# Holding back the first stores of an all-to-all dispatch kernel with a GpSimd copy

## The chip, the cores and the metric

The kernel runs on one core of a Trainium2 chip. The metric is the time of one execution on the device in microseconds (us). Before the change the median of three runs is 239.9 us (239.7 to 240.48).

The core has a matrix engine (TensorE, not used here), VectorE (DVE in the profile), ScalarE (ACT), GpSimd (POOL) and SyncE (SP). 16 DMA engines move data between HBM and the on-chip memory SBUF, which has 128 partitions. SP and ScalarE each have a DMA queue here; a transfer is issued by an instruction in the stream of the engine that owns the queue.

## The reference

Each of 16 x 1024 = 16384 tokens has a row of 512 float32 values and two weights. The output holds each row twice, once times each weight. The expert indices are an input and are not used.

```python
x_expanded = x[:, :, np.newaxis, :].repeat(k, axis=2)   # k = 2
weights = expert_weights[..., np.newaxis]
return (x_expanded * weights).astype(np.float32)
```

So 33.5 MB of x and 0.13 MB of weights are read, and 67.1 MB are written.

## The kernel before

Each of the 128 partitions handles 128 tokens. They are cut into five tiles of 25 tokens per partition and a last small one of 3. "Token" below means one token in each of the 128 partitions: 256 KB of x, 512 KB of output.

**Memory.** Two buffers of 25 tokens hold x (tile 0, 2 and 4 use the one, tile 1 and 3 the other), `z_tile` holds x of the last 3 tokens, `w_tile` holds all weights, and one buffer `o_ring` holds the output of one whole tile. All later tiles write into the same `o_ring`, so a part of it can be computed again only when its earlier store has landed.

**Products.** A tile is done in two halves, of 13 and 12 tokens. In `fill` VectorE takes the first tokens of a half (9 in tile 0, 8 later), four tokens an instruction (line 116), and ScalarE the others, one output row of 512 an instruction (line 106). When a half is done, SP issues its store (line 141).

**Loads.** ScalarE's queue carries x (line 79). Tile 0 comes in two steps of 9 and 16 tokens. Tile 1 is issued right behind, but in the compiled order its issue waits until the first 9 tokens have landed. Tile 2 is issued when both engines are done with tile 0. The load of the three last tokens (line 87) stands behind tile 2's load on ScalarE's queue; a one-column copy (line 76), which writes `z_tile` and reads the last column of `o_ring`, keeps it behind tile 0's products. Tile 3 and 4 are issued when their buffers are free.

**Weights.** SP's queue carries six loads of weights (line 93), one for each tile and one for the last three tokens, all issued at the start. The stores go into the same queue behind them. Each weight load is 128 pieces of 200 bytes (24 bytes for the last three tokens).

The order of each engine's instructions is the order of the program; semaphores between engines and DMAs are put in by the framework from the overlaps of the buffers.

Of the kernel before, what the change touches and what calls it, by code (L numbers as in the profile page):

```python
# [1 line left out]

# [4 lines left out]


@with_exitstack
def kernel(  # L10
    ctx: ExitStack,
    tc: tile.TileContext,
    x: bass.AP,
    expert_indices: bass.AP,
    expert_weights: bass.AP,
    out: bass.AP,
):
    nc = tc.nc

    batch, seq, hidden = x.shape  # L20
    k = expert_weights.shape[-1]
    P = nc.NUM_PARTITIONS
    ntok = batch * seq
    assert ntok % P == 0
    A_TOTAL = ntok // P

    f32 = mybir.dt.float32
    row = k * hidden
    CH = 4


    groups = [25, 25, 25, 25, 25]
    TX = max(groups)
    LAST = 3
    FIRST = [9, 16]
    SHARES = [[9, 9], [8, 8]]
    assert sum(groups) + LAST == A_TOTAL

    xf = x.rearrange("b s h -> (b s) h")
    of = out.rearrange("b s k h -> (b s) (k h)")  # L40
    wf = expert_weights.rearrange("b s k -> (b s) k")

    w_pool = ctx.enter_context(tc.tile_pool(name="w_pool", bufs=1))
    x_pool = ctx.enter_context(tc.tile_pool(name="x_pool", bufs=2))
    o_pool = ctx.enter_context(tc.tile_pool(name="o_pool", bufs=1))

    w_tile = w_pool.tile([P, A_TOTAL * k], f32)
    o_ring = o_pool.tile([P, TX * row], f32)

    def rows(of_all, done, T):  # L50
        return of_all[done * P : (done + T) * P, :].rearrange(
            "(p a) n -> p (a n)", a=T
        )


    if LAST:
        z_pool = ctx.enter_context(tc.tile_pool(name="z_pool", bufs=1))
        z_tile = z_pool.tile([P, LAST * hidden], f32)

    tiles = []  # L60
    done = 0
    for n in groups:
        tiles.append((done, n))
        done += n

    loaded = []

    def load(i):
        if i >= len(tiles):
            return  # L70
        done, n = tiles[i]
        x_tile = x_pool.tile([P, TX * hidden], f32)
        src = rows(xf, done, n)
        steps = FIRST if i == 0 else [n]
        if i == 2 and LAST:
            nc.scalar.copy(out=z_tile[:, :1], in_=o_ring[:, TX * row - 1 :])  # L76
        for e, step in enumerate(steps):
            at = sum(steps[:e])
            nc.scalar.dma_start(  # L79
                out=x_tile[:, at * hidden : (at + step) * hidden],  # L80
                in_=src[:, at * hidden : (at + step) * hidden],
            )
            if i == 0 and e == 0:
                for g in range(len(tiles) + 1):
                    weights(g)
        if i == 2 and LAST:
            nc.scalar.dma_start(out=z_tile, in_=rows(xf, A_TOTAL - LAST, LAST))
        loaded.append(x_tile)


    def weights(e):
        at, n = tiles[e] if e < len(tiles) else (A_TOTAL - LAST, LAST)
        nc.sync.dma_start(
            out=w_tile[:, at * k : (at + n) * k], in_=rows(wf, at, n)
        )

    def product(engine, o_tile, t, x_in, c, m):

        o = t * row
        if engine is not None:  # L100
            for e in range(m * k):
                out_e = o_tile[:, o + e * hidden : o + (e + 1) * hidden]
                in_e = x_in[:, e // k * hidden : (e // k + 1) * hidden]
                w_e = w_tile[:, c + e : c + e + 1]
                if engine is nc.scalar or engine is nc.any and (c + e) % 3 == 2:
                    nc.scalar.mul(out=out_e, in_=in_e, mul=w_e)  # L106
                else:
                    nc.vector.tensor_scalar(
                        out=out_e,
                        in0=in_e,  # L110
                        scalar1=w_e,
                        scalar2=None,
                        op0=mybir.AluOpType.mult,
                    )
            return
        nc.vector.tensor_tensor(  # L116
            out=o_tile[:, o : o + m * row].rearrange(
                "p (t k h) -> p t k h", t=m, k=k
            ),
            in0=x_in[:, : m * hidden]  # L120
            .rearrange("p (t h) -> p t h", t=m)
            .unsqueeze(2)
            .to_broadcast([P, m, k, hidden]),
            in1=w_tile[:, c : c + m * k]
            .rearrange("p (t k) -> p t k", t=m)
            .unsqueeze(3)
            .to_broadcast([P, m, k, hidden]),
            op=mybir.AluOpType.mult,
        )

    def fill(o_tile, x_in, c, m, v):
        for t in range(0, v, CH):
            u = min(t + CH, v)
            product(None, o_tile, t, x_in[:, t * hidden : u * hidden], c + t * k, u - t)
        product(nc.scalar, o_tile, v, x_in[:, v * hidden :], c + v * k, m - v)

    def emit(src, dst, c, cuts, shares):
        for at, to, v in zip(cuts, cuts[1:], shares):
            o_tile = o_ring[:, at * row : to * row]
            fill(o_tile, src[:, at * hidden : to * hidden], c + at * k, to - at, v)  # L140
            nc.sync.dma_start(out=dst[:, at * row : to * row], in_=o_tile)  # L141

    for i in range(2):
        load(i)
    for i, (done, n) in enumerate(tiles):
        emit(loaded[i], rows(of, done, n), done * k, [0, 13, n], SHARES[min(i, 1)])
        load(i + 2)
    emit(
        z_tile,
        rows(of, A_TOTAL - LAST, LAST),  # L150
        (A_TOTAL - LAST) * k,
        [0, LAST],
        [LAST],
    )

# [1 line left out]
_INS = ['x', 'expert_indices', 'expert_weights']  # L157
_OUTS = [((16, 1024, 2, 512), 'float32')]


# [23 lines left out]
```

## Time and profile before

| what | value |
|---|---|
| median of three runs | 239.9 us |
| profiled execution | 239.73 us |
| its span | 238.0 us |
| VectorE busy | 93.2 us |
| ScalarE busy | 55.2 us |
| GpSimd busy | 0.2 us |
| bytes moved by DMA | 100.80 MB |
| mean rate over the span | 424 GB/s |

The profile is that of one execution. Its span runs from the first to the last instruction on the core; the profiled execution's own time is 1.73 us longer than its span. The view of DMA issues gives the median time from issue to landing of a group of transfers, so a transfer that stands behind others in its queue shows a long time. In the 40-slice line a digit is the mean busy share of the 16 DMA engines in tenths. In the timeline each row has a start, a length, the engine (ending in q where the engine only issues a DMA), the line, the operation, and in brackets the idle time ahead of it with what ended it. A DMA view for a stretch of time counts the packets that moved in it by queue: q10 is ScalarE's queue, q1 is SP's.

### The profile page before, as it was taken

Reading aid. Unit: us, or ns where it says so; the run is one execution under the profiler, and the core shown is the slowest. Engines: PE = TensorE matmul, PEld = TensorE weight load, DVE = VectorE, ACT = ScalarE, POOL = GpSimd, SP = SyncE. Lnnn points to the kernel's source line nnn. Section 1 sums busy time; section 2 is a strip of 40 time slices with the busy share of each in tenths; the row PEclk is TensorE's granted clock in tenths of the full one; section 3 lists DMA queues with packets and bytes.
Section 4 is the critical chain, followed back from the end, with each engine's and each line's share of the span. In section 5 each row is a group of like instructions: output and inputs, shape, how many; then the busy total and the mean of one; then the engine's idle time right before and its main releaser. Section 6 shows DMA issues by size and latency. Waiting matters only on the chain.

```text
span 238.0 us, 214 instructions
## 1 busy us (share of the span) xinstructions
DVE 93.2 (39%) x23; ACT 55.2 (23%) x88; POOL 0.2 (0%) x4
## 2 busy tenths in 40 slices
DVE  0599800000059193086005902920085292861300
ACT  0008800000054170081005302700080280800000
POOL 0000000000000000000000000000000000000000
DMA  6999999999999999999999999999999999999996
GB/s 252 445 415 493 475 415 414 415 386 457 430 406 397 434 439 456 458 430 415 405 435 484 430 434 434 413 405 431 490 430 448 417 397 423 457 448 438 438 397 264
DMA packets 3457, 100.80 MB, mean 424 GB/s; under 512 B 1152, under 2 KB 1152, under 8 KB 1280
## 3 DMA queue, kind: packets, MB, share of 16 engines
q1 hardware_dynamic: 2448, 67.24, 65.5%
q10 hardware_dynamic: 1008, 33.55, 33.1%
q14 instruction: 1, 0.01, 0.0%
HBM read 33.69 MB, written 67.11 MB: 424 GB/s over the span
## 4 chain that ended last, share of the span: by engine, by line
DMA 69%; DVE 16%; issue 5%; ACT 3%; ACTq 0%; DVEq 0%; SPq 0%
DMA out_dram<-o_ring 62%; DVE o_ring L116 16%; DMA x_tile<-in_x_dram 7%; ACT o_ring L106 2%; ACT L106 1%; ACTq L79 0%; DVEq L116 0%; SPq L141 0%; ACTq L106 0%
## 5 line engine op out<-in xcount | busy, mean ns | idle before, releaser
L116 DVE TENSOR_TENSOR o_ring<-x_tile,w_tile 128x4096 f32<-128x4096 f32 (+1 forms) x22 | 89.8, 4130 | 122.4 <-DMA out_dram<-o_ring 102.8
L106 ACT ACTIVATE o_ring<-x_tile,w_tile 128x512 f32<-128x512 f32 x86 | 53.7, 708 | 134.4 <-DMA out_dram<-o_ring 134.4
L116 DVE TENSOR_TENSOR o_ring<-z_tile,w_tile 128x3072 f32<-128x3072 f32 x1 | 3.4, 3359 | 7.0 <-DMA out_dram<-o_ring 7.0
L106 ACT ACT_TABLE_LOAD x1 | 1.3, 1283 | 18.8 <-DMA x_tile<-in_x_dram 18.8
L76 ACT COPY z_tile<-o_ring 128x1 f32<-128x1 f32 x1 | 0.2, 191 | 0.0
L168 POOL MEMSET const-bfloat16-1.0<- 128x1 bf16 x1 | 0.1, 102 | 0.0
L168 POOL MEMSET const-uint8-127<- 128x1 uint8 x1 | 0.1, 102 | 0.0
L168 POOL MEMSET const-float32-1.0<- 128x1 f32 x1 | 0.1, 99 | 0.0
L168 POOL MEMSET const-float32-0.0<- 128x1 f32 x1 | 0.1, 98 | 0.2 <-issue 0.2
## 6 DMA issues: line engine op xcount, KB each, us to landing
out_dram<-o_ring SPq DMA_DIRECT2D x5, 6656.0 KB, 32.7
out_dram<-o_ring SPq DMA_DIRECT2D x5, 6144.0 KB, 36.4
x_tile<-in_x_dram ACTq DMA_DIRECT2D x4, 6400.0 KB, 29.7
x_tile<-in_x_dram ACTq DMA_DIRECT2D x1, 4096.0 KB, 17.6
x_tile<-in_x_dram ACTq DMA_DIRECT2D x1, 2304.0 KB, 8.1
out_dram<-o_ring SPq DMA_DIRECT2D x1, 1536.0 KB, 14.6
z_tile<-in_x_dram ACTq DMA_DIRECT2D x1, 768.0 KB, 10.5
w_tile<-in_expert_weights_dram SPq DMA_DIRECT2D x5, 25.0 KB, 24.7
```

The lines of the kernel that those rows point to most:

```text
L76: nc.scalar.copy(out=z_tile[:, :1], in_=o_ring[:, TX * row - 1 :])
L106: nc.scalar.mul(out=out_e, in_=in_e, mul=w_e)
L116: nc.vector.tensor_tensor(out=o_tile[:, o : o + m * row].rearrange("p (t k h) -> p t k h", t=m, k=k), in0=x_in[:, : m * hidden] .rearrange ...
L168: nc = _bacc.Bacc("TRN2", target_bir_lowering=False, num_devices=1)
```

## The change

Three things are changed.

1. The weights of tiles 0 and 1 stay on SP's queue. Those of tiles 2 and 3 (now one transfer), of tile 4 and of the last three tokens are issued on ScalarE's queue, behind tile 1's load.
2. Tile 2 is loaded in two steps, 23 tokens and then 2. It is now issued ahead of the one-column copy, and the load of the three last tokens follows the 2.
3. The two stores of tile 0 are issued only after three small GpSimd copies. The first reads a place that the load of the 23 tokens writes, so it waits until they are in; the second reads two columns of `o_ring`, one in each half, and the third writes the same values back. Each of them passes through the small buffer `hold`, so they run one after the other, and the stores, which read what the third wrote, wait for it.

The buffers of x are now named in a list instead of coming from a pool of two. In the compiled order tile 1's load no longer waits for the first 9 tokens. The products, the shares of the engines, the cuts into halves and all later stores and loads stay.

```diff
-    FIRST = [9, 16]
-    SHARES = [[9, 9], [8, 8]]
+    STEPS = {0: [9, 16], 2: [23, 2]}
...
+    hold = w_pool.tile([P, 2], f32)
+    x_pair = [x_pool.tile([P, TX * hidden], f32, name=f"x{e}") for e in range(2)]
+    z_tile = x_pool.tile([P, LAST * hidden], f32)
...
+    def load(i, e):
+        at = sum(STEPS.get(i, groups[i : i + 1])[:e])
+        to = at + STEPS.get(i, groups[i : i + 1])[e]
+        part = slice(at * hidden, to * hidden)
+        nc.scalar.dma_start(out=x_pair[i % 2][:, part], in_=rows(xf, *tiles[i])[:, part])
...
+    def weights(engine, g, to):
+        at, n = tiles[g]
+        engine.dma_start(
+            out=w_tile[:, at * k : (at + (to - g) * n) * k].rearrange(
+                "p (g m) -> p g m", g=to - g
+            ),
+            in_=wf[at * P : (at + (to - g) * n) * P, :].rearrange(
+                "(g p a) n -> p g (a n)", g=to - g, p=P
+            ),
         )
...
-    for i in range(2):
-        load(i)
+    load(0, 0)
+    weights(nc.sync, 0, 1)
+    weights(nc.sync, 1, 2)
+    load(0, 1)
+    load(1, 0)
+    weights(nc.scalar, 2, 4)
+    weights(nc.scalar, 4, 5)
+    nc.scalar.dma_start(
+        out=w_tile[:, (A_TOTAL - LAST) * k :], in_=rows(wf, A_TOTAL - LAST, LAST)
+    )
     for i, (done, n) in enumerate(tiles):
-        emit(loaded[i], rows(of, done, n), done * k, [0, 13, n], SHARES[min(i, 1)])
-        load(i + 2)
...
+        dst = rows(of, done, n)
+        halves = [(0, 13), (13, n)]
+        for at, to in halves:
+            make(x_pair[i % 2], done * k, at, to, 9 if i == 0 else 8)
+            if i > 0:
+                store(dst, at, to)
+        if i == 0:
+            nc.scalar.copy(out=z_tile[:, :1], in_=o_ring[:, TX * row - 1 :])
+            load(2, 0)
+            load(2, 1)
+            nc.scalar.dma_start(out=z_tile, in_=rows(xf, A_TOTAL - LAST, LAST))
+
+            nc.gpsimd.tensor_copy(out=hold, in_=x_pair[0][:, :2])
+            held = o_ring[:, : 13 * row + 1 : 13 * row]
+            nc.gpsimd.tensor_copy(out=hold, in_=held)
+            nc.gpsimd.tensor_copy(out=held, in_=hold)
+            for at, to in halves:
+                store(dst, at, to)
+        elif i + 2 < G:
+            load(i + 2, 0)
+    make(z_tile, (A_TOTAL - LAST) * k, 0, LAST, LAST)
+    store(rows(of, A_TOTAL - LAST, LAST), 0, LAST)
```

More of the change, by code (lines that the diff above doesn't have):

```diff
@@ L43 @@
     w_pool = ctx.enter_context(tc.tile_pool(name="w_pool", bufs=1))
-    x_pool = ctx.enter_context(tc.tile_pool(name="x_pool", bufs=2))
+    x_pool = ctx.enter_context(tc.tile_pool(name="x_pool", bufs=1))
     o_pool = ctx.enter_context(tc.tile_pool(name="o_pool", bufs=1))
     w_tile = w_pool.tile([P, A_TOTAL * k], f32)
+    hold = w_pool.tile([P, 2], f32)
     o_ring = o_pool.tile([P, TX * row], f32)
+    x_pair = [x_pool.tile([P, TX * hidden], f32, name=f"x{e}") for e in range(2)]
+    z_tile = x_pool.tile([P, LAST * hidden], f32)
     def rows(of_all, done, T):
@@ L53, in rows @@
         )
-    if LAST:
-        z_pool = ctx.enter_context(tc.tile_pool(name="z_pool", bufs=1))
-        z_tile = z_pool.tile([P, LAST * hidden], f32)
     tiles = []
@@ L64 @@
         done += n
[L66 to L94, printed above, removed]
+    def load(i, e):
[12 more added lines that the diff above has]
+            ),
         )
```

20 lines of the change are left out of this document (8 added, 12 removed).

## The prediction

> **What bounds the kernel now.** I read the page first, for who is busy and how many bytes move.
>
> ```profile
> span 238.0 us, 214 instructions
> DVE 93.2 (39%) x23; ACT 55.2 (23%) x88; POOL 0.2 (0%) x4
> DMA  6999999999999999999999999999999999999996
> ...
> DMA packets 3457, 100.80 MB, mean 424 GB/s; under 512 B 1152, under 2 KB 1152, under 8 KB 1280
> ...
> q1 hardware_dynamic: 2448, 67.24, 65.5%
> q10 hardware_dynamic: 1008, 33.55, 33.1%
> ...
> DMA 69%; DVE 16%; issue 5%; ACT 3%; ACTq 0%; DVEq 0%; SPq 0%
> ```
>
> VectorE and ScalarE are mostly idle. The 40-slice DMA line has no slice below 9 between its ends, and the two queues (q1 is SP's, q10 ScalarE's) fill 65.5 + 33.1 = 98.6% of 16 engines' span, 234.7 of 238.0 us. So the chain's "DVE 16%" is not a term of the sum: stores of the other half run meanwhile. The time is bytes over rate, plus moments in which the DMA engines have nothing queued or work badly. The bytes don't change, so only those moments can.
>
> Next the DMA issues and the timeline up to the first stores.
>
> ```profile
> out_dram<-o_ring SPq DMA_DIRECT2D x5, 6656.0 KB, 32.7
> out_dram<-o_ring SPq DMA_DIRECT2D x5, 6144.0 KB, 36.4
> x_tile<-in_x_dram ACTq DMA_DIRECT2D x1, 4096.0 KB, 17.6
> x_tile<-in_x_dram ACTq DMA_DIRECT2D x1, 2304.0 KB, 8.1
> w_tile<-in_expert_weights_dram SPq DMA_DIRECT2D x5, 25.0 KB, 24.7
> w_tile<-in_expert_weights_dram SPq DMA_DIRECT2D x1, 3.0 KB, 49.0
> ```
>
> ```profile
> 0.73 3.11 SPq L93 DMA_DIRECT2D w_tile<-in_expert_weights_dram  x6
> 0.73 8.50 ACTq L79 DMA_DIRECT2D x_tile<-in_x_dram  x3
> ...
> 18.79 1.28 ACT L106 ACT_TABLE_LOAD   x1 [18.79 <-DMA x_tile<-in_x_dram]
> 20.08 8.69 ACT L106 ACTIVATE o_ring<-x_tile,w_tile 128x512 f32<-128x512 f32 x14
> 25.12 197.72 SPq L141 DMA_DIRECT2D out_dram<-o_ring  x11
> 28.80 0.19 ACT L76 COPY z_tile<-o_ring 128x1 f32<-128x1 f32 x1
> 28.86 0.35 ACTq L79 DMA_DIRECT2D x_tile<-in_x_dram  x1
> 41.70 0.33 ACTq L87 DMA_DIRECT2D z_tile<-in_x_dram  x1
> ...
> 68.17 8.76 DVE L116 TENSOR_TENSOR o_ring<-x_tile,w_tile 128x4096 f32<-128x4096 f32 x2 [39.54 <-DMA out_dram<-o_ring]
> ```
>
> A 3 KB transfer that takes 49.0 us to land is the strange row. The weights are issued in SP's first 4 us, yet the last of them lands at about 52. The first store is issued at 25.12, behind them in the same queue. The DMA view by stretch shows what that means: 25 to 48 us, 48 to 52 and 52 to 90.
>
> ```profile
> DMA packets 416, 9.87 MB, mean 429 GB/s; under 512 B 224, under 2 KB 224, under 8 KB 224
> q10 hardware_dynamic: 208, 9.83, 98.9%
> q1 hardware_dynamic: 208, 0.04, 0.8%
> out_dram<-o_ring SPq DMA_DIRECT2D x1, 6656.0 KB, 42.9
> x_tile<-in_x_dram ACTq DMA_DIRECT2D x1, 6400.0 KB, 20.4
> z_tile<-in_x_dram ACTq DMA_DIRECT2D x1, 768.0 KB, 10.5
> ```
>
> ```profile
> DMA packets 416, 1.66 MB, mean 414 GB/s; under 512 B 272, under 2 KB 272, under 8 KB 400
> q10 hardware_dynamic: 160, 0.79, 63.2%
> q1 hardware_dynamic: 256, 0.87, 53.7%
> ```
>
> ```profile
> DMA packets 352, 16.52 MB, mean 435 GB/s; under 512 B 32, under 2 KB 32, under 8 KB 32
> q1 hardware_dynamic: 352, 16.52, 100.3%
> ```
>
> From 25 to 48 us SP's queue moved 0.04 MB in 208 packets, weights only, though a store had been issued at 25.12: small weight packets take turns with 50 KB packets of x, and the store stands behind them. **The stores of the first tile are held today already**, by accident, until the third tile is nearly in: it lands at 28.86 + 20.4 = 49.3, the three-token tile at 41.70 + 10.5 = 52.2. Nor is there a rate to win by separating reads from writes: reads alone run at 429 GB/s, stores alone at 435.
>
> The Trainium skill ("DMA: Bandwidth & Descriptors", section "Queues, rings and completion order") says that each DMA engine takes turns between its queues packet by packet, whatever their size. The trace agrees: 208 weight packets against 208 of x in that stretch.
>
> **The change, part by part.** The sum is made against the profiled execution: 238.0 of span and 1.7 around it, 239.73 us, 0.2 below the median of 239.9.
>
> *Loads.* x of tile 1 no longer waits for the first 9 tokens; they and the next 16 tokens are queued anyway: 0. Tile 2's load is issued, as now, when both engines are done with tile 0, at 20.08 + 8.69 = 28.8. Tile 1's load covers that until about 34.0 (tile 2's 6400 KB need 15.3 us at 429 GB/s before they are in at 49.3). That leaves some 4 us after the 1.0 from issue to first bytes (below); without that cover the loss would be what ScalarE is late. ScalarE's queue now issues six DMAs before its first product, some 0.35 us each by the rows above, all before 4 us; it waits until 18.79 for data. The two extra issues at 28.8 delay no product, since the next ones wait for a store until 68.
>
> *Weights.* The number of transfers and packets stays; four transfers of weights (tiles 2, 3, 4 and the last three tokens), 512 packets, move from SP's queue, where they alternate with x, into ScalarE's queue in one burst between tile 1 and tile 2. Interleaved, 208 cost 0.8% of 23 us = 0.18 us, 14 ns each on one of 16 engines, so 512 cost 0.45 us. In a burst: below, 0.45 us better if they vanish. Above, each packet stalls as the small three-token load does: that load took 63.2% of 4 us = 2.53 us for 0.79 MB that need 1.83 at 429 GB/s, 0.70 us over 8 packets per engine, 87 ns each; 32 packets per engine then cost 2.8 us, 2.35 more than now. The nearest row is the start, where the first weights run in bursts too:
>
> ```profile
> GB/s 0 0 0 0 0 0 5 331 228 151 150 379 149 671 373 373 523 297 447 671 75 664 516 75 745 373 150 670 373 299 745 148 667 1324 132 0 0 924 1055 131
> q1 hardware_dynamic: 240, 0.04, 2.9%
> ```
>
> In 0 to 10 us, 240 packets took 2.9% = 0.29 us, 19 ns each. At that price 512 cost 0.6 us, 0.15 more than now. I take +0.2, with the restart of x behind them.
>
> *The hold.* Tile 2 comes as 23 and 2 tokens. The 2 are 512 KB, 1.2 us at 429 GB/s, so the 23 are in at 49.3 - 1.2 = 48.1. Then three GpSimd copies, each waiting for the one before, and the first store's issue. Every store queues behind this on SP; VectorE's first product of tile 1 waits for the same copies and for the first store anyway; GpSimd has nothing else to do. What such a copy costs is not in the trace; the nearest rows are these.
>
> ```profile
> L116 DVE TENSOR_TENSOR o_ring<-x_tile,w_tile 128x1024 f32<-128x1024 f32 x2 | 2.4, 1216 | 0.0
> L168 POOL MEMSET const-float32-0.0<- 128x1 f32 x1 | 0.1, 98 | 0.2 <-issue 0.2
> ```
>
> Between 0.10 us (GpSimd's own memset) and 1.22 us (VectorE's smallest, with 512 times the elements); I take 0.2 like ScalarE's 128x1 copy (0.19), so 0.6 in all, 0.1 more for hand-over. From issue to first bytes it takes about 1.0 us (weights issued at 0.73, first bytes in the slice at 1.5 to 1.75). So store bytes start at 48.1 + 0.7 + 1.0 = 49.8; with the upper price 48.1 + 3.65 + 1.0 = 52.8. The cover is what stands in ScalarE's queue: 2 + 3 tokens, 1.31 MB, 3.05 us at full rate, until 51.1 at least. Idle time: 0, at the upper price 1.7 us. If nothing covered it, the hold would cost the whole 1.7 us.
>
> *Small loads.* The 2-token load adds 8 packets of 4 KB per engine to the 8 of 6 KB of the three-token load, the kind that wasted 0.70 us. Below: stores come early enough to fill those gaps, and 0.70 us is won. Above: the 2 tokens waste 0.70 as well. The hold lets about 1.7 us of small packets run alone, more than half of them: I take +0.4 for the 2 tokens and -0.2 for the three.
>
> *After that.* Stores begin about where they do now, each half (14 to 16 us) covers the 8.8 us of products of the other, and loads 3 and 4 are issued at the same places. Nothing is gained or lost: 0.
>
> Sum: 239.73 + 0.2 + 0 + 0.4 - 0.2 = 240.1 us: within what a measurement of this kernel can tell from no change (0.3%, 0.7 us: 239.2 to 240.6).
>
> **The rivals.**
> *Faster.* The store's packets come in before the small loads have stalled, and the burst is prefetched behind tile 1's big packets. The 0.70 and the 0.45 go: 239.73 - 1.15 = 238.6. For it: back-to-back weights were cheap at the start. Against: the small loads stand before the store for 1.7 us. It decides if the hold takes under 1 us.
> *The hold outlasts its cover.* GpSimd copies and their semaphores cost 1.2 us each: 1.7 idle and 0.4 of stalled small loads, 241.8. It decides above about 0.65 us a copy ((3.05 - 1.0 - 0.1) / 3). Against it: GpSimd's own 0.10.
> *The burst stalls.* 87 ns a packet instead of 14: 239.73 + 2.35 + 0.2 = 242.3. Against it: the first weights, 19 ns.
> *A small load pays for itself.* The three-token load lands 2.9 us after tile 2's, 1.1 more than its bytes need; the 2-token load pays 1.1 as well: 240.8. The Trainium skill speaks for this one ("DMA: Bandwidth & Descriptors", section "Rules for kernel authors"): it asks for 1 MiB or more per DMA, and this load has half of that. [...]
> *The change does not do what it says*, since the stores are held already: that is the forecast itself.
>
> **How the numbers follow.** Forecast 0.43 (no change); faster rival 0.19; hold too long 0.15; burst 0.12; small load 0.09; 0.02 for a cause that I don't see, shared by both sides. Faster 0.2, same 0.43, slower 0.37. The range runs from the faster rival's 238.6, a little inside it at 238.7, to 242.0, above the hold's 241.8; it leaves out the full burst and a part of the faster case, under 2 in 10.
>
> **What would show it.** Right: no slice below 9 in the DMA line around 48 to 52; the first store's issue some 0.7 us after the 23 tokens land; GpSimd copies of 0.1 to 0.3 us; tile 2's 23 tokens landing near 48; the first products of tile 1 starting near 67 instead of 68. Wrong: an idle stretch of the DMA engines ahead of the first store, or copies over 0.65 us (the hold); 23 tokens landing a microsecond or more later than 48 (the burst); a queue share of ScalarE above 33.1 + 0.4% (small loads); a sum of shares 0.4% below 98.6 with a shorter span (the faster rival). I would be wrong altogether if the rate of the stores alone or of the mixed stretches changed, since no step of mine touches it.

## The result and the profile after

The changed kernel takes 240.93 us (median of 8 runs, 240.64 to 241.61) against 239.87 us (median of 8, 239.61 to 240.48) for the kernel before: a ratio of 1.0045, 95% interval 1.0031 to 1.0058. It is slower by 0.45%. The forecast was 240.1 us and no change; the measured time lies inside its range, above the 239.2 to 240.6 us that counted as no change, on the side that had a chance of 0.37. The profiled execution took 240.83 us, 239.0 of them span. One run of the changed kernel with a delay, below, fell into a slower state (244.66 us) and is left out of its median and ratio.

From the page of the changed kernel, the lines that answer to the first ones above:

```profile
span 239.0 us, 218 instructions
...
DMA  6999998999999999999999999999999999999996
...
q1 hardware_dynamic: 1872, 67.16, 65.2%
q10 hardware_dynamic: 1712, 33.64, 33.4%
```

The DMA engines are as full as before: 65.2 + 33.4 = 98.6% of the span, now of 239.0 us instead of 238.0, for the same bytes. So the extra microsecond isn't a gap in front of the stores. Packets take longer somewhere.

The changed kernel's timeline around the hold:

```profile
28.72 0.33 ACTq L67 DMA_DIRECT2D x<-in_x_dram  x1
...
48.28 0.19 POOL L153 COPY hold<-x 128x2 f32<-128x2 f32 x1 [47.84 <-DMA x<-in_x_dram]
48.52 0.19 POOL L155 COPY hold<-o_ring 128x2 f32<-128x2 f32 x1
48.77 0.19 POOL L156 COPY o_ring<-hold 128x2 f32<-128x2 f32 x1
48.98 0.82 SPq L125 DMA_DIRECT2D out_dram<-o_ring  x2
```

The 23 tokens release GpSimd at 48.28 us, each copy takes 0.19 us, and the first store is issued 0.70 us after the release.

To find where the time goes I use VectorE's starts as milestones. Its first product of a half begins when the store that held that part of the output buffer has landed, so the starts say how far the DMA queues are. First the kernel before, then the changed one (start, length, engine, line, operation; in brackets the idle time ahead and what ended it). The row at 68.17 of the kernel before stands in the prediction.

```profile
82.57 8.76 DVE L116 TENSOR_TENSOR o_ring<-x_tile,w_tile 128x4096 f32<-128x4096 f32 x2 [5.64 <-DMA out_dram<-o_ring]
...
127.88 8.76 DVE L116 TENSOR_TENSOR o_ring<-x_tile,w_tile 128x4096 f32<-128x4096 f32 x2 [17.05 <-DMA out_dram<-o_ring]
...
173.18 8.76 DVE L116 TENSOR_TENSOR o_ring<-x_tile,w_tile 128x4096 f32<-128x4096 f32 x2 [17.13 <-DMA out_dram<-o_ring]
...
219.12 3.36 DVE L116 TENSOR_TENSOR o_ring<-z_tile,w_tile 128x3072 f32<-128x3072 f32 x1 [6.95 <-DMA out_dram<-o_ring]
```

```profile
67.33 8.76 DVE L99 TENSOR_TENSOR o_ring<-x,w_tile 128x4096 f32<-128x4096 f32 x2 [38.69 <-DMA out_dram<-o_ring]
...
81.68 8.76 DVE L99 TENSOR_TENSOR o_ring<-x,w_tile 128x4096 f32<-128x4096 f32 x2 [5.59 <-DMA out_dram<-o_ring]
...
128.41 8.76 DVE L99 TENSOR_TENSOR o_ring<-x,w_tile 128x4096 f32<-128x4096 f32 x2 [17.05 <-DMA out_dram<-o_ring]
...
174.25 8.76 DVE L99 TENSOR_TENSOR o_ring<-x,w_tile 128x4096 f32<-128x4096 f32 x2 [17.45 <-DMA out_dram<-o_ring]
...
220.20 3.36 DVE L99 TENSOR_TENSOR o_ring<-z_tile,w_tile 128x3072 f32<-128x3072 f32 x1 [6.97 <-DMA out_dram<-o_ring]
```

| milestone (us) | before | changed | difference |
|---|---|---|---|
| tile 1, first half | 68.17 | 67.33 | -0.84 |
| tile 1, second half | 82.57 | 81.68 | -0.89 |
| tile 2, second half | 127.88 | 128.41 | +0.53 |
| tile 3, second half | 173.18 | 174.25 | +1.07 |
| last three tokens | 219.12 | 220.20 | +1.08 |

The changed kernel is 0.9 us ahead when the first stores have landed. It then loses 1.42 us between the second halves of tiles 1 and 2 (46.73 us instead of 45.31) and another 0.54 us between those of tiles 2 and 3 (45.84 instead of 45.30). From there both run alike (45.94 and 45.95 us). The two stretches that lose are those in which the loads of tiles 3 and 4 meet the stores.

Call the first of these stretches **the first meeting**. Between the landing of tile 0's second store and that of tile 1's second store, 6656 + 6144 KB of output and 6400 KB of x go through, 19.7 MB. At the 435 GB/s of the stores alone that is 45.2 us. The kernel before needs 45.31, nothing to spare; the changed kernel needs 46.73. In the DMA view of the 15 us in which tile 3's load begins (90 to 105 us), of the kernel before and of the changed one:

```profile
DMA packets 141, 6.45 MB, mean 430 GB/s; under 512 B 16, under 2 KB 16, under 8 KB 16
q1 hardware_dynamic: 87, 3.69, 56.8%
q10 hardware_dynamic: 54, 2.76, 42.5%
```

```profile
DMA packets 132, 6.00 MB, mean 400 GB/s; under 512 B 16, under 2 KB 16, under 8 KB 16
q1 hardware_dynamic: 84, 3.54, 57.4%
q10 hardware_dynamic: 48, 2.46, 43.3%
```

In the second one the shares still add up to 100.7% (99.3% in the first): the engines were busy all the time and moved 400 GB/s. A packet of x took 1.89 us in the first (42.5% of 15 us on 16 engines, for 54 packets) and 2.16 us in the second.

More than half of the 0.9 us gained ahead of that comes from the small loads. From 48 to 51 us in the changed kernel:

```profile
q10 hardware_dynamic: 223, 1.04, 85.7%
```

1.04 MB in 85.7% of 3 us are 405 GB/s while they ran. The three-token load of the kernel before moved 0.79 MB in 2.53 us, 312 GB/s. So the small loads no longer stall. At 405 GB/s their 1.31 MB take 3.24 us; in the kernel before the three tokens took 2.53 us, and the other two, at the 429 GB/s of x, 1.22. That is 0.5 of the 0.9 us. A part of the rest lies in how a milestone is read (see the end of the experiments).

### The profile page after: what moved, and what is told of

Read it like the earlier page. It is cut to its first block, busy times and chain, and to the rows that moved or that the text cites. A ratio compares the mean times of both kernels' runs of the same rounds, so it can differ in the third digit from the quotient of the medians.

```text
span 239.0 us, 218 instructions
## 1 busy us (share of the span) xinstructions
DVE 93.1 (39%) x23; ACT 55.1 (23%) x88; POOL 0.8 (0%) x7
## 2 busy tenths in 40 slices
DMA packets 3585, 100.80 MB, mean 422 GB/s; under 512 B 1152, under 2 KB 1152, under 8 KB 1408
## 3 DMA queue, kind: packets, MB, share of 16 engines
q1 hardware_dynamic: 1872, 67.16, 65.2%
q10 hardware_dynamic: 1712, 33.64, 33.4%
## 4 chain that ended last, share of the span: by engine, by line
DMA 52%; issue 25%; DVE 16%; POOL 0%; POOLq 0%; DVEq 0%; SPq 0%
DMA out_dram<-o_ring 52%; DVE o_ring L99 16%; DVEq L99 0%; POOLq L187 0%; POOL hold L153 0%; POOL hold L155 0%; SPq L125 0%; POOLq L155 0%; POOLq L176 0%
## 5 line engine op out<-in xcount | busy, mean ns | idle before, releaser
L99 DVE TENSOR_TENSOR o_ring<-x,w_tile 128x4096 f32<-128x4096 f32 (+1 forms) x22 | 89.8, 4130 | 123.4 <-DMA out_dram<-o_ring 103.6
L89 ACT ACTIVATE o_ring<-x,w_tile 128x512 f32<-128x512 f32 x86 | 53.7, 708 | 135.2 <-DMA out_dram<-o_ring 135.2
```

What stands on the lines that cost most here:

```text
L99: nc.vector.tensor_tensor(out=o_tile[:, o : o + m * row].rearrange("p (t k h) -> p t k h", t=m, k=k), in0=x_in[:, : m * hidden] .rearrange ...
```

## The experiments

The measure of each is its time against the kernel before on the same chip, and the length of the first meeting, from the two rows of its timeline that are shown: the starts of tile 1's second half (near 82) and of tile 2's second half (near 128). In full-rate terms it is 45.2 us.

### Is it the same every time?

The changed kernel, run again.

> The changed kernel once more, unaltered, for a second trace. In step theory (when tile 3's load starts, most of the 16 DMA engines alternate between a packet of x and a packet of output at the same moment, and such packets take longer): again 13 or so of 16 engines take their first packet of tile 3 about 2 us after the others, and 90 to 105 us again moves about 400 GB/s against 430 before. Rival (a passing disturbance of one execution): the stretch moves 430 GB/s this time, and the time is still 240.9 us for another reason.

One run of 241.06 us, beside 239.69 us for the kernel before. Its DMA view from 90 to 105 us:

```profile
q1 hardware_dynamic: 84, 3.54, 57.1%
q10 hardware_dynamic: 48, 2.46, 43.9%
```

The same packets and bytes as in the first trace. The loss belongs to the kernel, not to one execution.

### Does the moment of tile 3's load matter?

Seven one-column copies on ScalarE between VectorE's last product of tile 1 and the issue of tile 3's load, in the changed kernel; and four in the kernel before.

```diff
         elif i + 2 < G:
+            for _ in range(7 if i == 1 else 0):
+                nc.scalar.copy(out=x_pair[i % 2][:, :1], in_=o_ring[:, 21 * row - 1 : 21 * row])
             load(i + 2, 0)
```

```diff
+        for _ in range(4 if i == 3 else 0):
+            nc.scalar.copy(out=x_tile[:, :1], in_=o_ring[:, 21 * row - 1 : 21 * row])
         for e, step in enumerate(steps):
```

> The changed kernel with seven one-column ScalarE copies between the end of tile 1's products and the issue of tile 3's load, some 1.7 us of delay; nothing else. In step theory: a packet takes 1.97 us, so a delay of 1.7 us puts the issue where about half of the engines take the load one packet earlier than the others, as in the kernel before; the long packets go, 90 to 105 us moves about 430 GB/s, and the time falls by about 1 us to 239.8 us. Rival (the moment does not matter; what stalls is the place in memory or the earlier start of the stores): 240.9 us, 90 to 105 us about 400 GB/s. If a later load simply cost its delay: 242.6 us.

> The kernel before with four such copies ahead of tile 3's load, some 1.0 us of delay. In step theory: half a packet later than now all engines take the load at the same packet, go in step, and the time rises by about 1.2 us to 241.1 us, with the rate from 90 to 107 us down from 430 to about 400 GB/s. Rival (the moment does not matter, the DMA engines are full anyway): 239.9 us and 430 GB/s. Both this and the delayed changed kernel have to come out as in step theory says for it to stand.

Changed kernel with the delay: 240.60 us (five runs), ratio 1.0047 (1.0033 to 1.0060). Its timeline, with the copies:

```profile
81.77 8.76 DVE L99 TENSOR_TENSOR o_ring<-x,w_tile 128x4096 f32<-128x4096 f32 x2 [5.62 <-DMA out_dram<-o_ring]
...
90.56 1.53 ACT L161 COPY x<-o_ring 128x1 f32<-128x1 f32 x7 [3.85 <-DVE o_ring L99]
...
128.63 8.76 DVE L99 TENSOR_TENSOR o_ring<-x,w_tile 128x4096 f32<-128x4096 f32 x2 [19.71 <-DMA out_dram<-o_ring]
```

The load goes out 1.5 us later, and the first meeting takes 46.86 us: the loss stays. Kernel before with the delay: 240.78 us, ratio 1.0043 (1.0028 to 1.0058).

```profile
82.28 8.76 DVE L118 TENSOR_TENSOR o_ring<-x_tile,w_tile 128x4096 f32<-128x4096 f32 x2 [5.64 <-DMA out_dram<-o_ring]
...
91.13 0.86 ACT L76 COPY x_tile<-o_ring 128x1 f32<-128x1 f32 x4 [3.91 <-DVE o_ring L118]
...
127.92 8.76 DVE L118 TENSOR_TENSOR o_ring<-x_tile,w_tile 128x4096 f32<-128x4096 f32 x2 [17.39 <-DMA out_dram<-o_ring]
...
174.82 8.76 DVE L118 TENSOR_TENSOR o_ring<-x_tile,w_tile 128x4096 f32<-128x4096 f32 x2 [18.73 <-DMA out_dram<-o_ring]
```

Here the first meeting takes 45.64 us, 0.33 more than without the delay and 1.1 less than in the changed kernel. The loss of the profiled execution (241.38 us, above the median; the runs spread from 239.79 to 241.66) is at the second meeting, with tile 4's load: 46.90 us against 45.30. So the two runs contradict the in-step theory, as it was put, at the place where it was to hold: the delay did not cure the changed kernel, and it did not bring the loss to tile 3's load in the other one. That a shifted load can make the kernel before 0.4% slower stands; in the one execution that was profiled it is lost at the next load.

### Where do the stores have to meet the loads without the hold?

The three GpSimd copies are left out of the changed kernel.

```diff
-            nc.gpsimd.tensor_copy(out=hold, in_=x_pair[0][:, :2])
-            held = o_ring[:, : 13 * row + 1 : 13 * row]
-            nc.gpsimd.tensor_copy(out=hold, in_=held)
-            nc.gpsimd.tensor_copy(out=held, in_=hold)
```

> The changed kernel without the three GpSimd copies: the first stores go out at about 25 us and alternate with the loads of tiles 1 and 2. In step theory: no fixed gain or loss from the hold as such; the three small loads then stand among stores and do not stall (0.6 us less than the kernel before), while the mixed stretch moves to 26 to 60 us and costs between 0 and 1.5 us by how the engines stand there: 239.3 to 241.0 us. Rival (reads and writes together are slow in themselves): over 241.5 us.

240.76 us, ratio 1.0048 (1.0031 to 1.0065): no better than with the hold. Stores and loads now meet at 25 us. The DMA view from 25 to 32 us:

```profile
DMA packets 48, 2.49 MB, mean 356 GB/s; under 512 B 0, under 2 KB 0, under 8 KB 0
q10 hardware_dynamic: 32, 1.64, 68.2%
q1 hardware_dynamic: 16, 0.85, 28.1%
```

Two packets of x per engine, 1.64 MB, took 68.2% of 7 us = 4.77 us, where 435 GB/s would need 3.77. One microsecond is lost there, at the first place where a large load and a large store meet. The rival that reads and writes are slow together throughout (over 241.5 us) falls.

### Is it where the buffers lie?

The small buffer takes 32 bytes per partition and moves all buffers behind it; the three-token buffer stands elsewhere too. Three kernels: the changed one with 64 bytes instead, the kernel before with 32 unused bytes, and the changed one with every buffer at the address of the kernel before.

```diff
-    hold = w_pool.tile([P, 2], f32)
+    hold = w_pool.tile([P, 16], f32)
...
```

```diff
     w_tile = w_pool.tile([P, A_TOTAL * k], f32)
+    spare = w_pool.tile([P, 2], f32)
+    nc.gpsimd.memset(spare, 0.0)
```

```diff
-    hold = w_pool.tile([P, 2], f32)
...
-    z_tile = x_pool.tile([P, LAST * hidden], f32)
+    z_pool = ctx.enter_context(tc.tile_pool(name="z_pool", bufs=1))
+    z_tile = z_pool.tile([P, LAST * hidden], f32)
+    hold = z_pool.tile([P, 2], f32)
```

(In the first of them the three copies then use `hold[:, :2]`.)

> The changed kernel with its small buffer made 16 columns wide instead of 2. In the changed kernel the buffer takes 32 bytes per partition, and the buffers of x and output behind it start 32 bytes off a multiple of 64; in the kernel before they start on one. With 64 bytes they do again. Place theory (an odd 32 bytes makes packets long where loads and stores alternate): the 1.2 us of long packets at 90 to 105 us go, that stretch moves about 430 GB/s, and since the changed kernel was 1.0 us ahead at 82 us the time is about 239.0 us. Rival (the moment at which the stores and loads meet, which this does not move): 240.9 us and 400 GB/s.

> The kernel before with two unused columns behind the weights (32 bytes), so that its buffers of x and output lie 32 bytes off a multiple of 64 as in the changed kernel; they are cleared once by GpSimd at the start. Place theory: long packets appear where tile 3's load meets the stores, 90 to 107 us falls from 430 to about 400 GB/s, and the time rises by 1 us or more to about 240.9 us. Rival (place does not matter): 239.8 us.

> The changed kernel with the three-token buffer and the small buffer behind the output, so that every buffer has exactly the address that it has in the kernel before; the work and its order are unchanged. Place theory, if it is the order or distance of the buffers and not the 64 bytes that counts: this one falls to about 239.0 us and the padded one does not; if it is the 64 bytes both do. Rival (the moment): both stay at 240.9 us.

In this order: 241.06 us, ratio 1.0060 (1.0044 to 1.0076); 239.78 us, 1.0003 (0.9994 to 1.0011); 240.86 us, 1.0049 (1.0034 to 1.0065). Their timelines, in the same order:

```profile
81.70 8.76 DVE L99 TENSOR_TENSOR o_ring<-x,w_tile 128x4096 f32<-128x4096 f32 x2 [5.62 <-DMA out_dram<-o_ring]
...
128.92 8.76 DVE L99 TENSOR_TENSOR o_ring<-x,w_tile 128x4096 f32<-128x4096 f32 x2 [17.04 <-DMA out_dram<-o_ring]
```

```profile
82.38 8.76 DVE L118 TENSOR_TENSOR o_ring<-x_tile,w_tile 128x4096 f32<-128x4096 f32 x2 [5.62 <-DMA out_dram<-o_ring]
...
127.91 8.76 DVE L118 TENSOR_TENSOR o_ring<-x_tile,w_tile 128x4096 f32<-128x4096 f32 x2 [17.45 <-DMA out_dram<-o_ring]
```

```profile
81.65 8.76 DVE L100 TENSOR_TENSOR o_ring<-x,w_tile 128x4096 f32<-128x4096 f32 x2 [5.59 <-DMA out_dram<-o_ring]
...
128.92 8.76 DVE L100 TENSOR_TENSOR o_ring<-x,w_tile 128x4096 f32<-128x4096 f32 x2 [17.39 <-DMA out_dram<-o_ring]
```

First meetings of 47.22, 45.53 and 47.27 us. The place theory falls on all three.

### Which part of the change brings it?

The weights back on SP's queue, the hold kept; a longer hold; tiles 3 and 4 in the other order; and the three-token load moved out of the hold into the middle of tile 0's second store.

```diff
-    weights(nc.sync, 1, 2)
+    for g in range(1, G):
+        weights(nc.sync, g, g + 1)
+    nc.sync.dma_start(
+        out=w_tile[:, (A_TOTAL - LAST) * k :], in_=rows(wf, A_TOTAL - LAST, LAST)
+    )
...
-    weights(nc.scalar, 2, 4)
-    weights(nc.scalar, 4, 5)
...
```

```diff
             nc.gpsimd.tensor_copy(out=hold, in_=held)
+            nc.gpsimd.tensor_copy(out=hold, in_=held)
+            nc.gpsimd.tensor_copy(out=hold, in_=held)
+            nc.gpsimd.tensor_copy(out=hold, in_=held)
```

```diff
+    base = list(tiles)
+    tiles[3], tiles[4] = tiles[4], tiles[3]
...
-        at, n = tiles[g]
+        at, n = base[g]
```

```diff
             if i > 0:
                 store(dst, at, to)
+            if i == 1 and at == 0:
+                nc.scalar.copy(out=z_tile[:, :1], in_=o_ring[:, 13 * row - 1 : 13 * row])
+                nc.scalar.dma_start(out=z_tile, in_=rows(xf, A_TOTAL - LAST, LAST))
```

(In the first one ScalarE's load of the last three tokens' weights goes as well. In the last one the copy and the load of x at the old place are left out.)

> The changed kernel with all six loads of weights back on SP's queue, issued at the start as in the kernel before; the hold, the 23 and 2 tokens and all else stay. If the weights' move is what brings the long packets at tile 3's load: they go (excess under 0.2 us, 90 to 105 us about 430 GB/s), the small loads stall again as in the kernel before (0.7 us), and the time is 239.8 us. If the hold brings them: they stay, the stall comes on top, and the time is 241.3 us or more.

> The changed kernel with three more GpSimd copies in the hold, 0.24 us each, so that the first stores begin about 0.7 us later, at 51.0 us as in the kernel before (50.9). If the long packets come from the moment at which the stores begin and meet tile 3's load: they go, and the time is 240.0 us in spite of the longer hold. If not: they stay, the queue is empty for up to 0.3 us ahead of the stores, and the time is 240.9 to 241.3 us.

> The changed kernel with tiles 3 and 4 in the other order, so that other addresses of x are read while the stores of tile 1 go out; amounts, buffers and order of the work are unchanged. Address theory (the place in HBM that is read and the place that is written fall on each other): the long packets at 90 to 105 us change by more than half, the time goes to 239.5 to 240.3 us. If the addresses do not matter: 240.9 us, about 1.2 us of long packets there.

> The changed kernel with the load of the last three tokens issued behind the first half of tile 1's products, at about 73 us, in the middle of tile 0's second store, instead of behind the 23 and 2 tokens. First-meeting theory (about 1 us is lost where a queue of loads and a queue of stores first meet in earnest, wherever that is: at the small loads in the kernel before, at tile 3's load in the changed one): packets at 73 to 80 us become long and those at 90 to 105 us do not, total about the same, 240.9 us. If not: the long packets stay at 90 to 105 us; the hold is now covered by 2 tokens alone, so the DMA engines are empty for about 1 us ahead of the first store, and the time is 241.5 to 242 us.

In this order: 241.13 us, ratio 1.0064 (1.0037 to 1.0092); 241.76 us, 1.0078 (1.0063 to 1.0093); 240.69 us, 1.0037 (1.0023 to 1.0052); 242.64 us, 1.0116 (1.0087 to 1.0145). The timelines:

```profile
81.83 8.76 DVE L99 TENSOR_TENSOR o_ring<-x,w_tile 128x4096 f32<-128x4096 f32 x2 [5.68 <-DMA out_dram<-o_ring]
...
129.18 8.76 DVE L99 TENSOR_TENSOR o_ring<-x,w_tile 128x4096 f32<-128x4096 f32 x2 [17.79 <-DMA out_dram<-o_ring]
```

```profile
81.74 8.76 DVE L99 TENSOR_TENSOR o_ring<-x,w_tile 128x4096 f32<-128x4096 f32 x2 [5.61 <-DMA out_dram<-o_ring]
...
129.27 8.76 DVE L99 TENSOR_TENSOR o_ring<-x,w_tile 128x4096 f32<-128x4096 f32 x2 [18.06 <-DMA out_dram<-o_ring]
```

```profile
81.72 8.76 DVE L102 TENSOR_TENSOR o_ring<-x,w_tile 128x4096 f32<-128x4096 f32 x2 [5.60 <-DMA out_dram<-o_ring]
...
128.64 8.76 DVE L102 TENSOR_TENSOR o_ring<-x,w_tile 128x4096 f32<-128x4096 f32 x2 [17.22 <-DMA out_dram<-o_ring]
```

```profile
81.77 8.76 DVE L99 TENSOR_TENSOR o_ring<-x,w_tile 128x4096 f32<-128x4096 f32 x2 [6.53 <-DMA out_dram<-o_ring]
...
129.89 8.76 DVE L99 TENSOR_TENSOR o_ring<-x,w_tile 128x4096 f32<-128x4096 f32 x2 [17.07 <-DMA out_dram<-o_ring]
```

First meetings of 47.35, 47.53, 46.92 and 48.12 us; the last one holds a part of the three-token load as well (0.79 MB in all, 1.8 us at full rate), so it can't be compared to the others to a few tenths.

The DMA views of two of them answer what was expected of the small loads: from 48 to 51 us with the weights on SP's queue, and from 48 to 52 us with the three-token load moved away. In a DMA view each packet counts in the slice of time in which it starts.

```profile
q10 hardware_dynamic: 222, 1.04, 86.5%
```

```profile
DMA  9699695452100000000999000000000000000000
```

What follows: moving the weights is not the cause, since the loss stays without it. The stall that was expected to come back with the weights did not: 1.04 MB in 86.5% of 3 us are 401 GB/s. Nor are the addresses of x that tile 3's load reads, as far as a whole tile's shift can show. The longer hold costs nothing up to 82 us (81.74 against 81.68: the small loads cover it) and yet 0.8 us in the end, all of it at the meeting; 241.76 us is above both times that were expected. The first-meeting theory in its strict form, that about a microsecond is paid once, wherever load and store first meet, is not borne out: with the three-token load put among tile 0's stores the loss at tile 3's load stayed. The empty time that was expected ahead of the first store with a cover of 2 tokens is there: in slices of 0.1 us, no packet starts between 49.1 and 49.9 us. The milestone near 82 does not show it, since the three tokens are no longer in front of the stores.

### The hold alone

The kernel before, with nothing but the hold: tile 0's two stores issued behind three GpSimd copies that wait for tile 2's load.

```diff
...
-        emit(loaded[i], rows(of, done, n), done * k, [0, 13, n], SHARES[min(i, 1)])
+        emit(loaded[i], rows(of, done, n), done * k, [0, 13, n], SHARES[min(i, 1)], i == 0)
         load(i + 2)
+        if i == 0:
+            nc.gpsimd.tensor_copy(out=hold, in_=loaded[2][:, :2])
+            both = o_ring[:, : 13 * row + 1 : 13 * row]
+            nc.gpsimd.tensor_copy(out=hold, in_=both)
+            nc.gpsimd.tensor_copy(out=both, in_=hold)
+            for at, to in ((0, 13), (13, n)):
+                nc.sync.dma_start(
+                    out=rows(of, done, n)[:, at * row : to * row],
+                    in_=o_ring[:, at * row : to * row],
+                )
```

(The last argument of `emit` leaves its stores out. `hold` lies behind `o_ring`.)

> The kernel before with the hold alone: tile 0's two stores are issued after three GpSimd copies that wait for tile 2's load (in one piece). Weights, loads and their waits stay as in the kernel before, so the first store bytes still begin near 51 us, behind the last weights. If the hold as such brings the long packets at tile 3's load: 1.2 us of them appear at 90 to 105 us, and the time is 241.0 us. If what brings them is the rest of the change (tile 1's load without its wait, or tile 2 in two pieces): 90 to 105 us stays at 430 GB/s, and the time is 239.8 us.

241.63 us, ratio 1.0084 (1.0070 to 1.0098). Its timeline, and its DMA view from 48 to 51 us:

```profile
81.98 8.76 DVE L117 TENSOR_TENSOR o_ring<-x_tile,w_tile 128x4096 f32<-128x4096 f32 x2 [5.77 <-DMA out_dram<-o_ring]
...
129.90 8.76 DVE L117 TENSOR_TENSOR o_ring<-x_tile,w_tile 128x4096 f32<-128x4096 f32 x2 [17.82 <-DMA out_dram<-o_ring]
```

```profile
q10 hardware_dynamic: 160, 0.79, 64.8%
```

The first meeting takes 47.92 us, 2.6 more than in the kernel before: the hold, without the rest of the change, brings the loss, and more of it than the 1.2 us expected. And it takes the small load's stall away: the three-token load, with the same weights beside it, took 64.8% of 3 us = 1.94 us, where the kernel before needs 2.53. So what slowed that load in the kernel before was neither its size nor the weights beside it alone. What the hold took from it is the stores that stood issued behind the weights at that time; that they are the reason is argued, since no run changes them alone. One more thing differs: the load's own issue comes earlier, at 29.39 us by the timeline of this kernel instead of 41.70, though in both it stands behind tile 2's load. For the loss this does not matter: the kernel in which that load goes out only at 72.80 us, above, has the hold and the loss too (48.12 us; with all 1.8 us of the three tokens taken off still 46.3).

```profile
29.39 0.39 ACTq L88 DMA_DIRECT2D z_tile<-in_x_dram  x1
```

The last column is explained below the table.

| kernel | ratio to before | tile 1, second half | first meeting | spread of the engines |
|---|---|---|---|---|
| before | 1 | 82.57 | 45.31 | 0.99 |
| before, 32 bytes | 1.0003 | 82.38 | 45.53 | 0.87 |
| before, delay | 1.0043 | 82.28 | 45.64 | 0.83 |
| changed | 1.0045 | 81.68 | 46.73 | 0.63 |
| changed, delay | 1.0047 | 81.77 | 46.86 | 0.56 |
| changed, tiles swapped | 1.0037 | 81.72 | 46.92 | 0.59 |
| changed, 64 bytes | 1.0060 | 81.70 | 47.22 | 0.55 |
| changed, same addresses | 1.0049 | 81.65 | 47.27 | 0.50 |
| changed, weights on SP | 1.0064 | 81.83 | 47.35 | 0.83 |
| changed, longer hold | 1.0078 | 81.74 | 47.53 | 0.21 |
| before, hold | 1.0084 | 81.98 | 47.92 | 0.16 |

Every kernel with the hold is 0.6 to 0.9 us ahead of the kernel before at 82 us and loses 1.4 to 2.6 us at the first meeting; none of the three without it in this table does (the changed kernel with the hold left out loses its microsecond earlier, at 25 to 32 us). By which path an early hold makes packets long 40 us later is open. The delays of the load that were tried, the addresses in SBUF, the weights, and a whole tile's shift in HBM are excluded by the runs above.

One thing that could carry it over these 40 us is in the traces: how far the 16 engines stand apart. Tile 0's second store is 128 packets of 48 KB, eight for each engine, and from 79 to 81 us the last 16 of them start. In the DMA view the window has 40 slices of 0.05 us, and one such packet in a slice reads as 983. The kernel before, then the one with the hold alone:

```profile
GB/s 0 0 0 0 0 0 2949 0 0 0 983 983 1966 2949 983 983 0 0 0 983 1966 0 0 0 0 0 983 0 0 0 0 0 0 0 0 0 0 0 0 0
```

```profile
GB/s 0 0 0 0 0 0 0 0 0 0 5898 3932 3932 1966 0 0 0 0 0 0 0 0 0 0 0 0 0 0 0 0 0 0 0 0 0 0 0 0 0 0
```

The 16 starts spread over 1.0 us in the first and 0.2 in the second. The table's last column has this spread, in us, from the packet records of each trace; in the kernel before and in the changed one it had the same value (0.99 and 0.63) some 28 us earlier, when the first store began. With one exception the kernels whose engines stand close together lose, and the closest two lose most. The exception is the changed kernel with the weights on SP's queue: 0.83 us, as in the kernel before with the delay, and yet 47.35 us against 45.64. And the second meeting does not follow the spread with which it begins: 1.17 us goes with 46.90 us in the kernel before with the delay, 1.27 with 45.38 in the one with the hold alone. So the spread is not shown to be the cause; no run changes it alone, and the profile doesn't say which engine a packet is on.

The spread also bears on the milestones, for a store has landed only when the slowest engine is through. By the mean end of these 16 packets the changed kernel is 0.70 us ahead of the kernel before, not 0.89, and the one with the hold alone 0.12, not 0.59. From there to the end of tile 1's second store the same means give 45.36 us before, 46.59 changed and 47.17 with the hold alone: the loss is there, with 1.2 and 1.8 us instead of 1.4 and 2.6.

## Why the prediction came out as it did

*What bounds the kernel, and that the stores are held already*: right. The rates of the pure stretches are what they were, and the span is bytes over rate plus moments of bad work.

*Loads, 0*: right. Tile 2's load is issued at 28.72 us, and ScalarE's six early issues delayed nothing.

*Weights, +0.2*: right, as far as the milestones show. The number of packets stayed, as the step says (1152 under 512 B in both kernels); the number of transfers did not, since tiles 2 and 3 share one. The 23 tokens were to be in at 48.1; they released GpSimd at 48.28. With the weights back on SP's queue the time is no better (1.0064 against 1.0045, intervals overlapping), so the move costs little.

*The hold, 0.7 us and no idle time*: right in its size. Three copies of 0.19 us (0.2 was taken) and 0.70 us from release to issue. The first store's bytes started at 50.3 us instead of 49.8. Three more copies left the milestone at 82 us where it was (81.74 against 81.68), so the cover was enough.

*Small loads, +0.4 and -0.2*: wrong in its sign. The step read the three-token load's 87 ns a packet as the price of a small packet and added it for the 2 tokens. Both loads together moved at 405 GB/s, and at 82 us the kernel was 0.89 us ahead where the sum had it 0.4 behind. The hold alone took most of that stall away with the weights left in place. The faster rival was right that most of the 0.70 us would go, and its reason was wrong: the loads did not stall though they ran ahead of the store. The small-load rival falls; that its 240.8 us lies next to the measured 240.93 is chance. The Trainium skill's 1 MiB rule ("DMA: Bandwidth & Descriptors", section "Rules for kernel authors") showed little here: a load of 512 KB and one of 768 KB behind others in a queue ran at 93% (405 of 435) of the full rate.

*After that, 0*: the step that failed, with the small loads. It took the later stretches as fixed because their bytes, issues and covers were. By the milestones they cost 1.96 us more in the profiled execution (1.42 at the first meeting, 0.54 at the second), with the engines busy from 90 to 105 us (100.7%), where they moved 400 instead of 430 GB/s. The hold alone brings such a loss; by which path is open. The prediction named it as what would make it wrong altogether, a changed rate in the mixed stretches, and gave it no rival and no chance of its own. All its signs for being right came true, down to tile 1's first products at 67.33 us; they end at 68 us, ahead of the loss. The sum then is 239.73 - 0.89 + 1.96 = 240.8 us, the profiled 240.83.

The chance of 0.43 for no change was too high: the three slower rivals that held 0.36 each had another cause. That the time lies in the range is luck: the range was drawn wide for them, and a gain and a loss that the sum did not have left 1.1 us over.

## What to carry to other kernels

Where the DMA engines are full from end to end, don't take the stretches behind a change as fixed: mark milestones through the whole trace of both kernels and subtract, since a gain early on can be given back where loads and stores meet again. A transfer that is slow in one place need not be slow by its size; look at what else stands issued in the queues at that moment before its price is used elsewhere. And where stores are already held back by what stands ahead of them in their queue, an explicit wait has little to win.

## What was not expected of the hardware

The engines can be busy for the whole of a stretch and move 400 instead of 430 GB/s with the same kinds of packets (57.4 + 43.3% of 15 us, 6.00 MB instead of 6.45). Whether that happened at tile 3's load went with how the stores had been issued some 40 us earlier: 45.3 to 45.6 us in three kernels without the hold, 46.7 to 47.9 in eight with it. The spread of the 16 engines when the first store began, 0.99 us in the kernel before and 0.63 in the changed one, was the same at the end of tile 0's second store, some 28 us later.
